# Folded output weights of a pooling mixer: split into float32r pairs when they are folded, two blocks before they are used

## The chip, the cores and the metric

The kernel runs on one core of one Trainium2 chip. The core has a matrix engine (PE in the profile, with its weight loads as PEld), a vector engine (DVE), a scalar engine (ACT), a general engine (POOL) and a sequencer that only issues transfers (SP). POOL and ACT can issue transfers too. The metric is device time of one execution in microseconds; the median of three runs of the kernel before is 907.18 us (906.41 to 909.01).

## The reference, cut to what matters

Inputs are x (4096 rows of 1024, float32) and the weights of one layer, a pooling mixer:

```python
normed = rms_norm(x, norm_w)
u, gate = split(normed @ in_w)                  # 1024 -> 2 x 1024
for g, win in enumerate((2, 4, 8, 16)):         # four groups of 256 channels
    pooled[g] = trailing_mean(u[g], win) - u[g]
    mixed[g] = pooled[g] @ group_w[g] + group_b[g]
y = mixed * scale * silu(gate)
h = x + y @ out_w
out = rms_norm(h, final_norm_w)
```

The float32 product is kept accurate by splitting each operand into a high part, rounded to the matrix engine's fast type float32r, and a low part, the rest. A product then takes three passes: high x high, high x low, low x high.

## The kernel before

Every large product is done by a seven-product scheme (Strassen in Winograd's form). The seven products are named P1 to P7. Each has its own weight matrix, a sum of quarters of the real weight, and its own operand, a sum of quarters of the activations, and the results are added up in PSUM banks or in SBUF. The order of the products is P1, P2, P7, P6, P5, P4, P3 in the input phases and P1, P7, P6, P2, P5, P4, P3 in the output phase.

There are three phases. In the first input phase ("a") one half of the input projection is done for four blocks of 1024 rows. In the second ("b") the other half is done for the same four blocks, with the operands that phase a stored to DRAM (`sd`). In the output phase ("o") the gated result, stored to DRAM as `yd`, goes through the output weight in eight blocks of 512 rows. A step is one product of one block. In phase b a step is 48 matrix instructions of 512 columns, but for P7 of blocks 1 to 3, which is itself split into seven small products (`product_seven`, line 745).

The list `steps` holds all steps, and the loop at line 1887 walks through it: it issues loads some steps ahead (`advance("load", ...)`), splits the operand of the next step or two (`split_step`), issues the matrix instructions and the read-out of the banks (`run`, `evict_in`), and then the extra work of that step. A scheduler with a model of its own decides how these instructions stand on each engine; `issue_after` bounds it. Each engine and each transfer queue works strictly in its order.

All loads and most temporaries share 11 slots named `st` and 8 named `vt`, 512 KB each (128 partitions x 4 KB). `take()` hands out the slot that was given back longest ago, and an instruction that writes into a slot waits until the last reader of the slot's old contents is done, a store to DRAM included. `ops` are four buffers for operands that are split, two a step. `w[i]` is the split weight of product i, 2 MB in two halves; it is the input weight until phase b ends, the output weight after it.

`out_w` is brought in during phase b. In block 1 `load_wo(0)` loads four quarters of one half of the rows after step P7, and `make_wo(0)` in step P6 scales them by `scale` (`scale_rows`, 8 ACT instructions) and stores seven folded matrices (`combine`: four DVE instructions; `store_weights`: seven stores to `wod` on SP). Block 2 does the same for the other half. In block 3, the last of phase b, as each product's input weight has been used for the last time, `load_w` loads the two halves of its output weight from `wod` (SP) and splits them (`split`: one ACT copy, one DVE subtraction) into `w[i]`. Pooling (`pool`, the running sums on DVE) is done a step or more after the projection that feeds it. In phase o some products are again split in seven with weights made from `wod[P2]` and `wod[P7]` (`load_inner`, `sum_inner`, `split_weight`).

In the row listings below `st8_97`, `op1_86` and the like are buffers (slot name and a running number), `sd2_1_1` is the saved operand of block 2, product 1, second half, `pair5_0` is the pair of product 5, first half, and the number of columns stands last.

Of the kernel before, what the change touches and what calls it, by code (L numbers as in the profile page):

```python
# [10 lines left out]
F32 = mybir.dt.float32  # L11
F32R = mybir.dt.float32r
# [3 lines left out]
P = 128  # L16
D = 1024
S = 4096
H = 512
TB = 1024  # L20
NB = S // TB
# [10 lines left out]
P1, P2, P3, P4, P5, P6, P7 = range(1, 8)  # L32
# [54 lines left out]
def kernel(  # L87
# [45 lines left out]
    dram = ctx.enter_context(tc.tile_pool(name="dram", bufs=1, space=bass.MemoryType.DRAM))  # L133
# [54 lines left out]
    def give(ap):  # L188
        next(p for p in (st, vt, early, early5) if id(ap) in p.used).give(ap)

    def add(dst, a, b):
        vector.tensor_tensor(out=dst, in0=a, in1=b, op=ALU.add)

    def sub(dst, a, b):
        return vector.tensor_tensor(out=dst, in0=a, in1=b, op=ALU.subtract)
# [4 lines left out]
    def copy(dst, src, func=AF.Copy):  # L200
        return scalar.activation(dst, src, func)

    def split(dst, src):

        latest_copy[0] = copy(dst[:, 0], src).ins
        latest_split[0] = sub(dst[:, 1], src, dst[:, 0].bitcast(F32)).ins

    latest_split, latest_copy = [None], [None]
# [9 lines left out]
    t3d = [dram.tile([P, 2, H], F32, name=f"t3d{h}") for h in range(2)]  # L218
    wod = {
        i: [dram.tile([P, 2, H], F32, name=f"wod{i}_{h}") for h in range(2)]  # L220
        for i in range(P1, P7 + 1)
    }
    sd = [
# [42 lines left out]
    def load_rows(mat, k, c):  # L266
        u = take()
        sync.dma_start(
            out=u, in_=mat[k * P : (k + 2) * P, c : c + H].rearrange("(t p) c -> p t c", p=P)
        )  # L270
        return u
# [9 lines left out]
    def scale_rows(u, cs):  # L281
        for j in range(2):
            scalar.activation(u[:, j], u[:, j], AF.Copy, scale=cs[j])
# [6 lines left out]
    def combine(b11, b21, b12, b22):  # L290

        sub(b12, b22, b12)
        add(b11, b12, b11)
        sub(b21, b21, b11)
        t1 = take()
        sub(t1, b22, b11)
        return {P6: b11, P7: b12, P5: t1, P4: b21, P3: b22}

    def pair(cs, h, kh):
        k = 4 * kh + 2 * h  # L300
        return cs[k : k + 2]

    def store_weights(dst, h, b11, b21, b12, b22):
        sync.dma_start(out=dst[P1][h], in_=b11)
        sync.dma_start(out=dst[P2][h], in_=b21)
        for i, u in combine(b11, b21, b12, b22).items():
            sync.dma_start(out=dst[i][h], in_=u)
            give(u)

# [66 lines left out]
    def load_wo(h):  # L376
        for n in range(2):
            for kh in range(2):
                raw_wo[kh, n] = load_rows(out_w, 4 * kh + 2 * h, n * H)

    def make_wo(h):
        us = dict(raw_wo)
        for (kh, n), u in us.items():
            scale_rows(u, pair(scale_c, h, kh))
        store_weights(wod, h, us[0, 0], us[1, 0], us[0, 1], us[1, 1])

    def load_w(src, i):
        for h in range(2):
            u = take()
            sync.dma_start(out=u, in_=src[i][h])  # L390
            with tc.issue_after(evicted[0]):
                split(w[i][h], u)
            give(u)

    latest = [None]

# [81 lines left out]
    sums, held = {}, {}  # L478
# [621 lines left out]
    ev, evicted, copied = {}, [None], []  # L1100
# [567 lines left out]
    def pool_later(n):  # L1668
        kind, b, i = steps[n]
        if i == P4:  # L1670
            args = (b, 0 if kind == "a" else 1, 1, ev.pop("22"), ev.pop("21"))
            wait = int(b == 0) if kind == "a" else 1 if b < NB - 1 else 2
        elif i == P3:
            args = (b, 0 if kind == "a" else 1, 0, ev.pop("12"), ev.pop("11"))
            wait = 1 + int(b == 0) if kind == "a" else 2 if b < NB - 1 else 5
        else:
            return
        pending.append((n + wait, args))

    def pool_due(n):  # L1680
        while pending and pending[0][0] <= n:
            pool(*pending.pop(0)[1])
# [169 lines left out]
    def advance(what, n, f, reach):  # L1852
        while at[what] + 1 < own_from and at[what] + 1 <= n + reach(*steps[at[what] + 1]):
            at[what] += 1
            f(at[what])
# [31 lines left out]
    for n in range(2, len(steps)):  # L1887
        kind, b, i = steps[n]
        ahead = kind == "a" and b + 1 < NB
        keep[0] = 5 if kind == "b" and b == NB - 1 else 3  # L1890
        advance("load", n, load, load_reach)
        if ahead:
            rows, squares = row_plan(b)
# [73 lines left out]
        if kind in ("a", "b"):  # L1967
            pool_later(n)
            if kind == "a":
                pool_due(n)  # L1970
            if kind == "b" and b == NB - 1:
                for p in {P1: (), P2: (), P7: (P1,), P6: (P2, P7), P5: (P6, P5)}.get(i, (i,)):
                    load_w(wod, p)
            if kind == "b" and b in (1, 2) and i == P7:
                load_wo(b - 1)
            if kind == "b" and b in (1, 2) and i == P6:
                with tc.issue_after(evicted[0]):
                    make_wo(b - 1)
            if kind == "b" and b == NB - 1 and i == P3:
                f = take("p (a b) -> p a b", a=2)  # L1980
                sync.dma_start(
                    out=f.rearrange("p a b -> p (a b)"), in_=final_w.partition_broadcast(P)
                )
                fw.append(f)
# [52 lines left out]
```

## Time and profile before

| | |
|---|---|
| median of three runs | 907.18 us |
| the profiled execution | 907.14 us, of which the span is 905.3 us |
| granted TensorE clock, mean | 0.998 |
| transfers | 203.30 MB, mean 225 GB/s |
| PE, DVE, ACT, POOL busy | 99%, 81%, 57%, 16% of the span |
| phase b, block 1: steps P6 to the end of block 2's P2 | 427.0 to 489.2 us |
| phase b, block 2: P6 to the end of block 3's P2 | 498.8 to 561.0 us |

The profile is one execution, taken by the hardware profiler. Times are microseconds from the start of the span. A busy figure is the union of an engine's instructions; those of the matrix engine are pipelined and overlap, so gaps shorter than one matrix instruction do not show as idle, while the distance from one instruction to the next still does. In a timeline row stand the start, the length, the engine, the line, the operation, what it writes and reads (buffer numbers left out) and the count; idle time ahead of it and what ended it stand in brackets. Nearly all DVE, ACT, POOL and SP rows carry line 79, a helper that records every call.

### The profile page before, as it was taken

The page shows a single profiled execution, that of the slowest core. Times are in us where ns is not written, and L with a number is a line of the kernel's source. Part 1 is how long each engine was busy: PE and PEld are TensorE (multiplying, and loading weights), DVE is VectorE, ACT ScalarE, POOL GpSimd, SP SyncE. Part 2 cuts the span into 40 slices and gives each one's busy share as a digit, 9 for nine tenths or more (in the row PEclk, how much of TensorE's full clock was granted, in tenths as well). Part 3 has the DMA queues.
Part 4 walks back from the last instruction along what each step waited for, and adds up shares of the span by engine and source line. Part 5 has one row for each costly group of instructions (what it writes and reads, how often), then busy time and mean ns, then how long its engine had stood idle before and what let it go on. Part 6 is the DMA issues. An engine that isn't in the chain of part 4 may idle for free.

```text
span 905.3 us, 12421 instructions
## 1 busy us (share of the span) xinstructions
PE 894.6 (99%) x4554; PEld 791.7 (87%) x4554; DVE 736.8 (81%) x910; ACT 518.6 (57%) x848; POOL 147.3 (16%) x244
## 2 busy tenths in 40 slices
PE   9999999999999999999999999999999999999996
PEld 7888888888888888889889889888889898998996
DVE  3899896984996997694596497699898878888798
ACT  7869547446445465346545644855557466565464
POOL 0031110110111000100010011011132343342430
PEclk9999999999999999999999999999999999999999
DMA  9989779677769565245574574756673855945953
GB/s 339 402 313 320 263 279 314 219 299 286 270 248 363 180 236 183 94 163 190 212 244 175 202 262 142 269 188 204 206 220 81 221 176 142 240 143 138 264 179 116
DMA packets 77756, 203.30 MB, mean 225 GB/s; under 512 B 7296, under 2 KB 25088, under 8 KB 77696
## 3 DMA queue, kind: packets, MB, share of 16 engines
q1 hardware_dynamic: 57872, 143.77, 46.0%
q0 software_dynamic: 19104, 57.69, 20.7%
q10 hardware_dynamic: 720, 1.06, 0.3%
q8 instruction: 35, 0.57, 0.3%
q14 instruction: 25, 0.20, 0.1%
HBM read 130.13 MB, written 72.36 MB: 224 GB/s over the span
## 4 chain that ended last, share of the span: by engine, by line
PE 50%; DVE 21%; DMA 10%; issue 6%; ACT 3%; POOL 1%; SPq 0%; DVEq 0%; POOLq 0%; ACTq 0%
PE bank L799 44%; DVE vt L79 8%; DVE st L79 6%; DVE op L79 5%; PE bank L745 3%; DMA vt<-yd 3%; PE bank L941 3%; DMA st<-wvd 2%; ACT op L79 1%; DMA st<-yd 1%; DVE w L79 1%; DMA out<-vt 1%; ACT vt L79 1%; DMA st<-wod 1%; DMA vt<-rd 1%
## 5 line engine op out<-in xcount | busy, mean ns | idle before, releaser
L799 PE MATMUL bank<-op,w 128*128 128x512 f32 x2544 | 550.6, 379 | 0.2 <-ACT st L79 0.2
L799 PEld LDWEIGHTS bank<-op,w 128*128 128x128 f32 x2544 | 480.4, 189 | 68.9 <-ACT st L79 0.6
L799 PE MATMUL bank<-w,op 128*128 128x512 f32 (+1 forms) x1044 | 230.5, 377 | 0.0
L799 PEld LDWEIGHTS bank<-w,op 128*128 128x128 f32 x1044 | 192.3, 189 | 25.0
L79 DVE TENSOR_TENSOR op<-st,op 128x1024 fp32r<-128x1024 f32 x120 | 145.9, 1220 | 60.1 <-ACT op L79 59.7
L79 ACT ACTIVATE op<-st 128x1024 fp32r<-128x1024 f32 x120 | 125.8, 1052 | 86.4 <-PE bank L799 31.2
L79 ACT ACTIVATE op<-vt 128x1024 fp32r<-128x1024 f32 x65 | 68.3, 1053 | 63.0 <-DVE vt L79 40.6
L79 ACT ACTIVATE vt<-bank 128x512 f32<-128x512 f32 (+1 forms) x122 | 67.4, 577 | 43.9 <-PE bank L799 37.8
L79 DVE TENSOR_TENSOR op<-vt,op 128x1024 fp32r<-128x1024 f32 x65 | 78.4, 1218 | 14.2 <-ACT op L79 14.1
L79 DVE TENSOR_TENSOR st<-st,st 128x1024 f32<-128x1024 f32 (+1 forms) x47 | 51.3, 1104 | 31.6 <-ACT st L79 16.8
L79 ACT ACTIVATE bank<-bank 128x512 f32<-128x512 f32 (+1 forms) x84 | 41.1, 490 | 53.1 <-PE bank L799 39.5
L79 POOL COPY vt<-tails 128x32 f32<-128x32 f32 x14 | 17.0, 1219 | 301.4 <-ACT tails L79 130.3
L79 ACT ACTIVATE st<-bank 128x512 f32<-128x512 f32 (+1 forms) x62 | 35.6, 588 | 37.5 <-PE bank L799 22.7
L79 DVE TENSOR_TENSOR vt<-bank,vt 128x512 f32<-128x512 f32 (+1 forms) x90 | 51.3, 596 | 6.0 <-PE bank L941 4.6
L79 ACT ACTIVATE st<-st 128x1024 f32<-128x1024 f32 x34 | 35.8, 1055 | 28.6 <-DVE st L79 27.1
L79 DVE TENSOR_TENSOR st<-bank,st 128x512 f32<-128x512 f32 (+1 forms) x72 | 43.7, 622 | 6.0 <-PE bank L941 3.1
L79 POOL DMA_DIRECT2D sd<-st x45 | 24.0, 535 | 125.1 <-DVE st L79 77.9
L941 PEld LDWEIGHTS bank<-w,op 128*128 128x128 f32 x312 | 40.4, 191 | 1.7
L79 DVE TENSOR_TENSOR st<-st,vt 128x1024 f32<-128x1024 f32 (+1 forms) x34 | 39.1, 1168 | 2.7 <-DMA vt<-rd 2.4
L941 PE MATMUL bank<-w,op 128*128 128x256 f32 x312 | 41.1, 275 | 0.0
L79 DVE TENSOR_TENSOR vt<-vt 128x1024 f32<-128x1024 f32 (+3 forms) x43 | 38.2, 890 | 0.2
L79 DVE TENSOR_TENSOR_SCAN vt<-vt,window 128x1040 f32<-128x1040 f32 x16 | 37.7, 2374 | 0.6 <-DMA wod<-vt 0.5
(118 smaller groups left out, 768.5 us busy)
## 6 DMA issues: line engine op xcount, KB each, us to landing
sd<-st POOLq DMA_DIRECT2D x45, 512.0 KB, 4.2
st<-sd SPq DMA_DIRECT2D x42, 512.0 KB, 4.0
st<-in_xt SPq DMA_DIRECT2D x28, 512.0 KB, 7.4
st<-in_x SPq DMA_DIRECT2D x21, 512.0 KB, 7.9
yd<-st SPq DMA_DIRECT2D x20, 512.0 KB, 3.3
vt<-yd SPq DMA_DIRECT2D x17, 512.0 KB, 10.5
st<-wod SPq DMA_DIRECT2D x16, 512.0 KB, 5.1
out<-vt POOLq DMA_DIRECT2D x16, 512.0 KB, 3.5
```

Of the source, the lines that this page charges most:

```text
L79: r = f(*args, **kwargs)
L745: latest[0] = nc.tensor.matmul(cell(n, c).rearrange("p (a s) -> p a s", s=2), x1, x2, start=i == P1 and k + m == 0, stop=k == 1 and m == 2 ...
L799: latest[0] = nc.tensor.matmul(ps, a, b, start=start and n == 0, stop=stop and n == 2, skip_group_check=True).ins
L941: latest[0] = nc.tensor.matmul(ps, x1, x2, start=start and k + n == 0, stop=k == 1 and n == 2, skip_group_check=True,).ins
```

## The change

In blocks 1 and 2 of phase b, the folded matrices are split where they are folded. `store_pair` takes a fresh slot for the high part (an ACT copy), makes the low part on DVE (in place of the source, or in a second fresh slot for P1 and P2, whose source is still needed), and stores both to a new DRAM tensor `pairs_d` on POOL's queue. The plain `wod` copies stay for P2 and P7 alone. `load_wo` moves from step P7 to P2, the scaling, the pairs of P1 and P2 and the fold from P6 to P7, and the other five pairs stand in step P6. In block 3 `load_w` loads each half of the pair, 1 MB, straight into `w[i]` from POOL's queue, without ACT or DVE; most products are loaded one step later than before. The number of slots that `take` keeps back in that block is 3 and no longer 5.

```diff
-        for i in range(P1, P7 + 1)
+        for i in (P2, P7)
+    }
+    pairs_d = {
+        i: [dram.tile([P, 2, 2, H], F32, name=f"pair{i}_{h}") for h in range(2)]
+        for i in range(P1, P7 + 1)
     }
...
-    def store_weights(dst, h, b11, b21, b12, b22):
-        sync.dma_start(out=dst[P1][h], in_=b11)
-        sync.dma_start(out=dst[P2][h], in_=b21)
-        for i, u in combine(b11, b21, b12, b22).items():
-            sync.dma_start(out=dst[i][h], in_=u)
-            give(u)
+    def store_pair(i, h, u, spare=False):
+        hi = take()
+        lo = take() if spare else u
+        latest_copy[0] = copy(hi.bitcast(F32R), u).ins
+        latest_split[0] = sub(lo.bitcast(F32R), u, hi).ins
+        for v, t in enumerate((hi, lo)):
+            gpsimd.dma_start(out=pairs_d[i][h][:, v], in_=t)
+            if spare or v == 0:
+                give(t)
+
+    def store_weights(h, b11, b21, b12, b22):
+        sync.dma_start(out=wod[P2][h], in_=b21)
+        store_pair(P1, h, b11, True)
+        store_pair(P2, h, b21, True)
+        return combine(b11, b21, b12, b22)
+
+    def store_rest(h, sums):
+        sync.dma_start(out=wod[P7][h], in_=sums[P7])
+        for i in (P6, P5, P4, P3, P7):
+            store_pair(i, h, sums[i])
+            give(sums[i])
...
-    def load_w(src, i):
+    def load_w(i):
         for h in range(2):
-            u = take()
-            sync.dma_start(out=u, in_=src[i][h])
-            with tc.issue_after(evicted[0]):
-                split(w[i][h], u)
-            give(u)
+            gpsimd.dma_start(out=w[i][h], in_=pairs_d[i][h].bitcast(F32R))
...
-        keep[0] = 5 if kind == "b" and b == NB - 1 else 3
+        keep[0] = 3
...
-                for p in {P1: (), P2: (), P7: (P1,), P6: (P2, P7), P5: (P6, P5)}.get(i, (i,)):
-                    load_w(wod, p)
-            if kind == "b" and b in (1, 2) and i == P7:
-                load_wo(b - 1)
-            if kind == "b" and b in (1, 2) and i == P6:
+                for p in {P1: (), P2: (P1,), P7: (P2,), P6: (P7,), P5: (P6,), P4: (P5,), P3: (P4, P3)}[i]:
+                    load_w(p)
+            if kind == "b" and b in (1, 2):
                 with tc.issue_after(evicted[0]):
-                    make_wo(b - 1)
+                    if i == P2:
+                        load_wo(b - 1)
+                    elif i == P7:
+                        folded = make_wo(b - 1)
+                    elif i == P6:
+                        store_rest(b - 1, folded)
```

How the instructions stand changes at three places that matter below. The first is ACT in block 1, right behind the read-out of step P7 (the four rows that read banks 0 to 3). Before, two operand copies and the read-out of step P6 (banks 4 to 7) come next, then the eight scalings:

```order
L79 ACTIVATE vt6_106<-bank3_72 128x512
L79 ACTIVATE op1_86<-st2_91 128x1024
L79 ACTIVATE op3_88<-st0_89 128x1024
L79 ACTIVATE st6_95<-bank4_73 128x512
L79 ACTIVATE st6_95<-bank5_74 128x512
L79 ACTIVATE st2_91<-bank6_75 128x512
L79 ACTIVATE st2_91<-bank7_76 128x512
L79 ACTIVATE vt1_101<-vt1_101,colt_114 128x512 x2
L79 ACTIVATE st1_90<-st1_90,colt_114 128x512 x2
L79 ACTIVATE st8_97<-st8_97,colt_114 128x512 x2
L79 ACTIVATE st9_98<-st9_98,colt_114 128x512 x2
```

In the changed kernel the scalings and the high parts of P1 (into `st8`) and P2 (into `st5`) stand there, and the operand copies and the read-out of P6 behind them:

```order
L79 ACTIVATE st0_89<-st0_89,colt_114 128x512 x2
L79 ACTIVATE vt7_107<-vt7_107,colt_114 128x512 x2
L79 ACTIVATE vt2_102<-vt2_102,colt_114 128x512 x2
L79 ACTIVATE vt0_100<-vt0_100,colt_114 128x512 x2
L79 ACTIVATE st8_97<-st0_89 128x1024
L79 ACTIVATE st5_94<-vt7_107 128x1024
L79 ACTIVATE op1_86<-st2_91 128x1024
L79 ACTIVATE st6_95<-bank4_73 128x512
L79 ACTIVATE st6_95<-bank5_74 128x512
L79 ACTIVATE op3_88<-vt6_106 128x1024
L79 ACTIVATE op0_85<-st1_90 128x1024
L79 ACTIVATE st2_91<-bank6_75 128x512
```

So the scalings moved ahead of P6's read-out, and two copies were added.

The second place is POOL's queue in block 1, the stores of the pairs of P6, P5, P4, P3 and P7. Before, nothing but small copies for the pooling stands there. Now:

```order
L79 DMA pair6_0_137<-vt3_103 128x1024
L79 DMA pair6_0_137<-st0_89 128x1024
L79 COPY vt6_106<-tails_116 128x2x16
L79 DMA pair5_0_135<-st0_89 128x1024
L79 DMA pair5_0_135<-st9_98 128x1024
L79 DMA pair4_0_133<-st0_89 128x1024
L79 DMA pair4_0_133<-vt7_107 128x1024
L79 DMA pair3_0_131<-st9_98 128x1024
L79 DMA pair3_0_131<-vt0_100 128x1024
L79 DMA pair7_0_139<-st0_89 128x1024
```

Slot `st0` carries, one after the other, the low part of P6 and the high parts of P5, P4 and P7; slot `st9` the low part of P5 and then the high part of P3.

The third place is DVE at the end of block 1: the low part of P3 and, three rows on, that of P7 (from `st0`), the adds that read out step P4 (banks 0 to 3), the first running sum, and the low part of the second half of block 2's first operand (`op0` from `st9`). Before, with no weight among them:

```order
L79 SCALAR_TENSOR_TENSOR vt7_107<-vt6_106,window_3432 128x1040
L79 TENSOR_TENSOR st6_95<-bank0_69,st6_95 128x512
L79 TENSOR_TENSOR st6_95<-bank1_70,st6_95 128x512
L79 TENSOR_TENSOR op3_88<-st8_97,op3_88 128x1024
L79 TENSOR_TENSOR st2_91<-bank2_71,st2_91 128x512
L79 SCALAR_TENSOR_TENSOR vt3_103<-vt3_103,vt0_100 128x2x512
L79 TENSOR_TENSOR st2_91<-bank3_72,st2_91 128x512
L79 TENSOR_TENSOR op0_85<-st1_90,op0_85 128x1024
```

and now:

```order
L79 TENSOR_TENSOR vt0_100<-vt0_100,st9_98 128x1024
L79 TENSOR_TENSOR st6_95<-bank0_69,st6_95 128x512
L79 TENSOR_TENSOR st6_95<-bank1_70,st6_95 128x512
L79 TENSOR_TENSOR vt2_102<-vt2_102,st0_89 128x1024
L79 TENSOR_TENSOR st2_91<-bank2_71,st2_91 128x512
L79 TENSOR_TENSOR st2_91<-bank3_72,st2_91 128x512
L79 SCALAR_TENSOR_TENSOR vt0_100<-vt1_101,window_3450 128x1040
L79 SCALAR_TENSOR_TENSOR vt0_100<-vt0_100,vt1_101 128x2x512
L79 TENSOR_REDUCE window_3588<-vt6_106 128x1
L79 SCALAR_TENSOR_TENSOR st6_95<-vt0_100,colt_114,st6_95 128x512
L79 TENSOR_TENSOR op0_85<-st9_98,op0_85 128x1024
```

Both running sums (of step P5's result) stood ahead of P4's read-out adds before; they stand behind those adds and the low part of P7 now.

More of the change, by code (lines that the diff above doesn't have):

```diff
@@ L384, in make_wo @@
             scale_rows(u, pair(scale_c, h, kh))
-        store_weights(wod, h, us[0, 0], us[1, 0], us[0, 1], us[1, 1])
-    def load_w(src, i):
+        return store_weights(h, us[0, 0], us[1, 0], us[0, 1], us[1, 1])
+    def load_w(i):
         for h in range(2):
-            u = take()
-            sync.dma_start(out=u, in_=src[i][h])
-            with tc.issue_after(evicted[0]):
-                split(w[i][h], u)
-            give(u)
+            gpsimd.dma_start(out=w[i][h], in_=pairs_d[i][h].bitcast(F32R))
     latest = [None]
```

## The prediction

> **What bounds the kernel now.** I read the page first, then PE's own waits, then the busy time by stretch, then the timelines of block 1.
>
> ```profile
> span 905.3 us, 12421 instructions
> PE 894.6 (99%) x4554; PEld 791.7 (87%) x4554; DVE 736.8 (81%) x910; ACT 518.6 (57%) x848; POOL 147.3 (16%) x244
> ...
> PE bank L941 <- DVE vt L79: 1.8, 1, 1.8
> PE bank L1687 <- PEq L2022: 0.8, 1, 0.8
> PE bank L451 <- DMA early<-in_group_w: 0.3, 1, 0.3
> PE bank L451 <- DMA early<-in_wut: 0.2, 1, 0.2
> PE bank L799 <- ACT st L79: 0.2, 1, 0.2
> ```
>
> PE is busy for all but 10.7 us of the span, and its five waits come to 3.3 us. Since gaps shorter than an instruction hide in "busy", I checked its pace:
>
> ```profile
> 427.04 62.33 PE L799 MATMUL bank<-op,w 128*128 128x512 f32 x288
> 489.20 2.84 PE L745 MATMUL bank<-op,w 128*128 128x256 f32 x24
> 498.80 21.53 PE L799 MATMUL bank<-op,w 128*128 128x512 f32 x99
> ```
>
> Six steps of 48 instructions take 489.20 - 427.04 = 62.16 us: 10.36 us a step, 0.216 us an instruction, the same from one end to the other. So blocks 1 and 2 of phase b run at PE's pace: what DVE and ACT do there is free while operands come in time, and costs one for one once they are late. There is one place where they are late:
>
> ```profile
> 565.00:650.00 85.00, 85.00 (x419) 75.05 (x417) 74.53 (x77) 50.58 (x72) 10.10 (x10) 1.00 0.70 223
> 650.00:660.00 10.00, 10.00 (x48) 8.77 (x47) 8.72 (x12) 7.08 (x15) 3.90 (x13) 1.00 0.27 106
> 660.00:670.00 10.00, 9.91 (x61) 8.76 (x59) 9.93 (x14) 8.20 (x13) 4.34 (x6) 1.00 0.86 239
> 670.00:680.00 10.00, 8.31 (x44) 7.49 (x45) 9.99 (x18) 2.42 (x4) 1.77 (x2) 1.00 0.96 252
> ...
> 671.69 0.94 PE L941 MATMUL bank<-inner,op 128*128 128x256 f32 x6 [1.77 <-DVE vt L79]
> ...
> L79 DVE TENSOR_TENSOR w<-st,w 128x1024 fp32r<-128x1024 f32 x14 | 16.5, 1217 | 5.5 <-ACT w L79 5.5
> L79 ACT ACTIVATE w<-st 128x1024 fp32r<-128x1024 f32 x14 | 14.3, 1059 | 3.6 <-DMA st<-wod 2.1 <-PE bank L799 1.4
> ```
>
> The columns of a stretch are PE, PEld, DVE, ACT and POOL busy, clock, DMA share, GB/s. DVE carries 74.53 of 85 us and then nearly all of 660 to 680, and PE waits 1.77 us for it. The 14 weight splits are 16.5 us of that backlog.
>
> **What the change gains.** The 14 copies and 14 subtractions leave block 3. The backlog shrinks by 16.5 us of work against a wait of 1.77 us, so I count the whole wait as gone: -1.8 us. More is not there to win: what else PE waits for lies at the start of the program (1.5 us), and the end behind the last product is not touched.
>
> **What it adds in blocks 1 and 2.** Seven copies of 1.05 us on ACT and seven subtractions of 1.22 us on DVE a block, 14 stores on POOL and five fewer on SP. As mere work it fits:
>
> ```profile
> 425.00:440.00 15.00, 15.00 (x80) 13.39 (x80) 6.09 (x6) 10.04 (x16) 0.00 (x0) 1.00 0.41 140
> 440.00:455.00 15.00, 15.00 (x71) 13.15 (x70) 11.77 (x12) 7.56 (x12) 0.21 (x1) 1.00 0.83 302
> 455.00:470.00 15.00, 15.00 (x72) 13.12 (x71) 15.00 (x18) 7.24 (x10) 2.12 (x1) 1.00 0.75 250
> 470.00:485.00 15.00, 15.00 (x71) 13.15 (x70) 14.68 (x17) 5.47 (x9) 1.35 (x2) 1.00 0.40 146
> 485.00:500.00 15.00, 15.00 (x111) 14.26 (x110) 7.01 (x8) 10.59 (x20) 0.00 (x0) 1.00 0.65 217
> ```
>
> DVE has 8.9 us free before 440 and 3.2 before 455. But from 455 to 485 it has only 0.3 us free in 30: a subtraction that slips past 455 pushes all behind it. What makes them slip is the slots. Slot st0 is P6's low part, then P5's, P4's and P7's high part, and each use waits until the store of the one before has landed. The price of a landing is the main unknown:
>
> ```profile
> sd<-st POOLq DMA_DIRECT2D x45, 512.0 KB, 4.2
> st<-sd SPq DMA_DIRECT2D x42, 512.0 KB, 4.0
> ...
> DMA to landing us min/median/max: 2.9/4.1/12.6
> ...
> sd<-st POOLq DMA_DIRECT2D x9, 512.0 KB, 4.0
> ...
> sd<-st POOLq DMA_DIRECT2D x7, 512.0 KB, 6.5
> ```
>
> The same kind of store (512 KB, POOL's queue) lands in 4.2 us in the median and 2.9 at least; the last two rows are the stretches 100 to 140 (263 GB/s) and 180 to 220 (310 GB/s). I first walk the chain at 4.2.
>
> ```profile
> 428.77 1.08 ACT L79 ACTIVATE op<-st 128x1024 fp32r<-128x1024 f32 x1
> 438.10 1.32 ACT L79 ACTIVATE vt<-vt,colt 128x512 f32<-128x512 f32 x2
> 439.32 3.78 ACT L79 ACTIVATE st<-st,colt 128x512 f32<-128x512 f32 x6
> 442.99 1.05 ACT L79 ACTIVATE op<-vt 128x1024 fp32r<-128x1024 f32 x1
> ...
> 443.13 1.23 DVE L79 TENSOR_TENSOR st<-st,st 128x1024 f32<-128x1024 f32 x1 [8.39 <-ACT st L79]
> 444.27 1.22 DVE L79 TENSOR_TENSOR op<-vt,op 128x1024 fp32r<-128x1024 f32 x1
> 453.66 4.68 DVE L79 TENSOR_TENSOR_SCAN vt<-vt,window 128x1040 f32<-128x1040 f32 x2
> 464.04 1.40 DVE L79 SCALAR_TENSOR_TENSOR st<-vt,colt,st 128x512 f32<-128x512 f32 x2
> 484.07 1.22 DVE L79 TENSOR_TENSOR op<-vt,op 128x1024 fp32r<-128x1024 f32 x1
> ```
>
> Block 1. ACT is through with P7's read-out at 428.8. The eight scalings take 442.99 - 438.10 = 4.9 us: 433.7. P1's high part is ready at 434.7 and its store, from st8, lands at 439.0. The low part of P2 goes into st8, so DVE waits there, with everything behind it. Six subtractions, 1.13 us apart, bring P6's low part at 445.9. From there, with 0.1 us a hand-over: landed 450.2, P5 high 451.4, landed 455.7, P4 high 456.8, landed 461.1, P7 high 462.3, P7 low 463.5. Behind it on DVE, up to the low part of the second operand that block 2's P7 needs at once, stand 4 running sums (2.34 each), 9 instructions of 1024 columns (1.13 apart) and 12 of 512 (0.66): 27.5 us, so 491.0. PE wants it at 489.3; before, it was there at 485.3. **Stall 1.7 us.** Two smaller ones lie within it or beside it: block 2's first operand (its second half is loaded into st9 only when P3's high part has landed) comes 0.4 us late, and P6's read-out on ACT, now behind the scalings, ends at about 437.2 where P5 first writes that bank at 437.4, which I count as nothing.
>
> Block 2 runs the same chain in st6, from PE's 498.80. P6's low part comes at 517.8 (the operand copy ahead of it needs a buffer that P5's first half holds until 514.3). Then landed 522.1, P5 high 523.3, landed 527.6, P4 high 528.7, landed 533.0, P7 high 534.2, P7 low 535.4; a read-out add, two gates, a running sum and the subtraction after it (6.1 us) bring DVE to 541.5, and the first operand of block 3, whose slot st8 was P3's high part until about 535, has its low half at 542.7. PE wants it at 498.80 + 4 x 10.36 + 0.1 = 540.3: 2.4 us, and 0.3 more for its second half. **Stall 2.7 us.** Together 4.4.
>
> Each further microsecond of landing adds 4 us in block 1 (P1, P6, P5, P4) and 3 in block 2, where P1's is hidden by the wait for the buffer. At the least, 2.9 us, both stalls are gone; at 6.5 us they are 10.9 and 9.6. Which is nearer? Block 1 moved 140, 302 and 250 GB/s in the three stretches from 425 to 470; nine more stores of 0.5 MB in these 45 us make it (231 + 100) = 331 GB/s, above the stretch with 6.5. But there the stores stood in pairs, while in the chain one goes at a time. I take 4.8, nearer the median: 1.7 + 2.4 + 2.7 + 1.8 = 8.6 us.
>
> On this the Trainium skill speaks against me: "DMA: Bandwidth & Descriptors", section "Anatomy of one DMA — SWDGE (gpsimd) path", gives a transfer from POOL's queue about 2.0 us plus its bytes at 436 GB/s, an estimate of 3.2 us for 512 KB. By that both stalls vanish and the time is that of the first rival below. The trace has 4.2 in the median and 2.9 at least, so I go by the trace.
>
> **Costed at nothing.** SP issues 24 fewer transfers. The 14 loads of 1 MB stand in POOL's queue behind PE's last use of each weight in block 3. The tightest is P3's, issued as phase o begins and used six steps later; a step of phase o is 24 instructions, so that is 6 x 24 x 0.216 = 31 us, against 8.4 us at twice the 512 KB landing. Without the cover a late one would cost up to those 8.4 us. Behind them in POOL's queue wait copies for the pooling and phase o's adds from x, which come a step or more later.
>
> **Sum.** 907.14 for the profiled execution (its span 905.3 and 1.8 around it), which is the median of the runs, 907.18, to 0.04: 907.1 - 1.8 + 8.6 = 914 us.
>
> **Rivals.** (a) *The landings are hidden.* At 3 us a landing, or if DVE's slack of 4 us before block 2's P7 is larger than I count, nothing is late, and the wait at 671 is gone: 907.1 - 1.8 = 905.4. For it: the minimum of 2.9, and DVE's 8.4 us of idling ahead of 443.13 that the change fills. Against it: four landings in a row, and 30 us of full DVE behind them. (b) *The transfers choke.* 16 MB more go through; landings of 6.5 us give 20.5 us of stalls, 926. For it: 0.83 and 0.75 DMA share already in block 1. Against it: stalls stretch the time in which the bytes move, which relieves the queue. (c) *The wait at 671 stays,* because not DVE's work but the loading of `wod[P2]` sets it: 914 + 1.8 = 916. Against it: those loads wait for slots that DVE frees late. That the splits don't really leave block 3 is not a rival; the order shows 14 loads into the weights with no arithmetic behind them.
>
> **Numbers.** Forecast (stalls of 4 to 14 us) 0.62; (a) 0.24; (b) 0.07; (c) 0.07. The time is 914; the range, from (a) to nearly (b), is 905 to 925; the forecast's own is 909.5 to 920. A measurement here can tell about 0.3%, 2.7 us, from no change. Faster by more than that needs more than the 1.8 us there is to win: 0.04, left for an effect that I don't see. Within: most of (a) and the low end of the forecast, 0.24. Slower: 0.72.
>
> **What would show it.** Right: PE waits on DVE or ACT at block 2's P1 or P7 and at block 3's P1, some 2 to 6 us each; ACT copies of high parts that wait for stores to the pairs; no wait near 671. Wrong: PE's six steps of blocks 1 and 2 still take 62.2 us each; or DVE has caught up by 485; or PE waits in phase o for a weight that POOL loaded.

## The result and the profile after

The changed kernel takes 939.98 us in the median of 4 runs (937.69 to 942.53), the kernel before beside it 907.26: a ratio of 1.036 [1.032, 1.040], 33 us slower. The direction was forecast, but the time lies well outside the range of 905 to 925. The profiled execution took 937.69 us. These are the head of its page, and the view of what PE waited for (total, times, longest):

```profile
span 935.9 us, 12450 instructions
PE 907.2 (97%) x4554; PEld 797.9 (85%) x4554; DVE 738.1 (79%) x910; ACT 518.3 (55%) x848; POOL 166.2 (18%) x286
...
PE bank L815 <- ACT op L79: 7.6, 3, 4.0
PE bank L957 <- DVE st L79: 3.7, 1, 3.7
PE bank L815 <- DVE op L79: 3.6, 4, 1.9
PE bank L815 <- ACT bank L79: 3.5, 1, 3.5
```

The span grew by 30.6 us; DVE and ACT are as busy as before (736.8 and 518.6 us then), since the splits were only moved. All of PE's waits sum to 21.5 us now (3.3 before). That is 18.2 of the 30.6; nearly all the rest stands in PE's busy time, which grew by 12.6 (907.2 against 894.6) with the same 4554 instructions. So the matmuls themselves have become slower somewhere. PE's timeline shows where the time is lost (L815 is the main product, L761 the seven small products of phase b, L957 those of phase o, called its own product below):

```profile
427.36 43.03 PE L815 MATMUL bank<-op,w 128*128 128x512 f32 x198
473.43 0.48 PE L815 MATMUL bank<-op,w 128*128 128x512 f32 x1 [3.04 <-ACT op L79]
474.69 14.69 PE L815 MATMUL bank<-op,w 128*128 128x512 f32 x59 [0.78 <-DVE op L79]
492.88 9.70 PE L815 MATMUL bank<-op,w 128*128 128x512 f32 x30 [3.50 <-ACT bank L79]
502.41 2.84 PE L761 MATMUL bank<-op,w 128*128 128x256 f32 x24
...
512.91 41.60 PE L815 MATMUL bank<-op,w 128*128 128x512 f32 x192
558.55 0.80 PE L815 MATMUL bank<-op,w 128*128 128x512 f32 x1 [4.04 <-ACT op L79]
...
584.90 2.84 PE L761 MATMUL bank<-op,w 128*128 128x256 f32 x24
...
613.32 25.95 PE L815 MATMUL bank<-op,w 128*128 128x512 f32 x119 [1.86 <-DVE op L79]
639.10 51.96 PE L815 MATMUL bank<-w,op 128*128 128x512 f32 x240
...
700.74 1.65 PE L957 MATMUL bank<-inner,op 128*128 128x256 f32 x6 [3.73 <-DVE st L79]
```

Against the same places before (427.04, 489.20, 498.80, 560.97, 612.01, 671.69, end 905.3), with the waits of the timeline subtracted:

| stretch | before | after | more | of it waits | rest |
|---|---|---|---|---|---|
| six steps from block 1's P6 to block 2's P7 | 62.16 | 75.05 | 12.89 | 7.32 | 5.57 |
| seven small products of block 2 | 9.60 | 10.50 | 0.90 | 0.63 | 0.27 |
| six steps to block 3's P7 | 62.17 | 71.99 | 9.82 | 5.49 | 4.33 |
| block 3's P7 to phase o | 51.04 | 54.20 | 3.16 | 2.36 | 0.80 |
| phase o to its own product | 59.68 | 61.64 | 1.96 | 1.96 | 0 |
| from there to the end | 233.61 | 235.16 | 1.55 | | 1.55 |

Another 0.32 us lies ahead of block 1's P6. The "rest" is mostly the clock: in rows of 1 us, with the granted clock at 0.50 for some 19 us in which PE works behind four of the waits, 9.7 us are lost. The remainder goes with stopping and starting: a matmul that stands alone between two waits takes 0.48 us (at 473.43) where one in a row takes 0.216. In the view by stretches of 5 us (PE with its count, PEld, DVE, ACT, POOL, granted clock, DMA share, GB/s), 15 to 17 matmuls stand behind a wait where 25 stand at full clock:

```profile
475.00:480.00 5.00, 5.00 (x17) 4.04 (x16) 5.00 (x6) 3.05 (x7) 0.00 (x0) 0.66 0.99 349
480.00:485.00 5.00, 5.00 (x25) 4.38 (x24) 5.00 (x5) 1.16 (x2) 0.00 (x0) 1.00 0.36 145
...
490.00:495.00 5.00, 2.12 (x5) 1.76 (x6) 5.00 (x6) 2.51 (x3) 0.09 (x1) 0.71 0.73 244
495.00:500.00 5.00, 5.00 (x15) 4.04 (x15) 2.96 (x6) 1.65 (x2) 0.33 (x1) 0.61 0.97 313
```

What made block 2's first product late stands in the timelines of ACT, DVE and SP (SPq is SP's DMA queue):

```profile
453.57 1.06 ACT L79 ACTIVATE st<-st 128x1024 fp32r<-128x1024 f32 x1 [3.65 <-DMA pair<-st]
...
458.01 1.06 ACT L79 ACTIVATE st<-vt 128x1024 fp32r<-128x1024 f32 x1 [2.32 <-DMA pair<-st]
...
472.32 1.06 ACT L79 ACTIVATE op<-st 128x1024 fp32r<-128x1024 f32 x1 [5.01 <-DMA st<-sd]
...
491.28 1.06 ACT L79 ACTIVATE op<-st 128x1024 fp32r<-128x1024 f32 x1 [7.76 <-DVE st L79]
492.25 0.58 ACT L79 ACTIVATE bank<-bank 128x512 f32<-128x512 f32 x1
...
463.80 1.22 DVE L79 TENSOR_TENSOR vt<-vt,st 128x1024 fp32r<-128x1024 f32 x1
...
468.88 2.38 DVE L79 TENSOR_TENSOR_SCAN vt<-vt,window 128x1040 f32<-128x1040 f32 x1 [2.67 <-DMA pair<-vt]
...
465.59 6.13 SPq L79 DMA_DIRECT2D st<-sd  x2
```

The high parts of P5 and P4 wait for stores to land, as forecast. The load of the operand's second half is issued at 465.59, when the store of P3's high part has freed its slot, and the ACT copy that needs it starts at 472.32. A running sum on DVE waits 2.67 us for the store of P3's low part, whose `vt` slot it writes. And at 491.28 ACT has waited 7.76 us for the front sum, which DVE makes from operands for the seven small products, with the copy of a bank behind it (492.25) for which PE waits 3.50 us: a place that the prediction doesn't have.

### The profile page after: what moved, and what is told of

The parts are those of the page before. It is cut to its first block, busy times and chain, and to the rows that moved or that the text cites. A ratio compares the mean times of both kernels' runs of the same rounds, so it can differ in the third digit from the quotient of the medians.

```text
span 935.9 us, 12450 instructions
## 1 busy us (share of the span) xinstructions
PE 907.2 (97%) x4554; PEld 797.9 (85%) x4554; DVE 738.1 (79%) x910; ACT 518.3 (55%) x848; POOL 166.2 (18%) x286
## 4 chain that ended last, share of the span: by engine, by line
PE 68%; issue 11%; DVE 9%; DMA 9%; POOL 1%; ACT 1%; DVEq 0%; POOLq 0%; SPq 0%; ACTq 0%
PE bank L815 60%; PE bank L957 4%; DVE vt L79 4%; PE bank L467 3%; DVE st L79 3%; DVE op L79 3%; DMA st<-yd 2%; DMA pair<-st 2%; DMA st<-sd 1%; DMA vt<-yd 1%; DMA st<-wod 1%; DMA yd<-vt 1%; POOL pair L79 1%; PE bank L761 1%; ACT st L79 1%
## 5 line engine op out<-in xcount | busy, mean ns | idle before, releaser
L815 PE MATMUL bank<-op,w 128*128 128x512 f32 x2544 | 560.7, 383 | 14.7 <-ACT op L79 7.6
L815 PEld LDWEIGHTS bank<-op,w 128*128 128x128 f32 x2544 | 485.1, 191 | 88.7 <-ACT op L79 9.1
L815 PE MATMUL bank<-w,op 128*128 128x512 f32 (+1 forms) x1044 | 231.2, 378 | 0.0
L815 PEld LDWEIGHTS bank<-w,op 128*128 128x128 f32 x1044 | 192.9, 190 | 25.2
L79 DVE TENSOR_TENSOR op<-vt,op 128x1024 fp32r<-128x1024 f32 x66 | 80.3, 1220 | 21.2 <-ACT op L79 21.2
L79 DVE TENSOR_TENSOR st<-st,st 128x1024 f32<-128x1024 f32 (+2 forms) x41 | 45.5, 1128 | 31.9 <-DMA st<-yd 13.6
L79 DVE TENSOR_TENSOR vt<-bank,vt 128x512 f32<-128x512 f32 (+1 forms) x111 | 62.1, 590 | 9.4 <-PE bank L957 3.8
L79 ACT ACTIVATE st<-st 128x1024 f32<-128x1024 f32 (+2 forms) x40 | 41.3, 1034 | 33.6 <-DVE st L79 23.9
L79 POOL COPY vt<-tails 128x32 f32<-128x32 f32 x14 | 12.9, 920 | 196.4 <-ACT tails L79 106.8
L957 PEld LDWEIGHTS bank<-w,op 128*128 128x128 f32 x312 | 40.3, 191 | 1.9 <-ACT bank L79 0.3
L957 PE MATMUL bank<-w,op 128*128 128x256 f32 x312 | 41.2, 275 | 0.0
L79 DVE TENSOR_TENSOR st<-st,vt 128x1024 f32<-128x1024 f32 (+2 forms) x31 | 36.0, 1183 | 6.3 <-DMA st<-wod 3.4
L79 DVE TENSOR_TENSOR st<-bank,st 128x512 f32<-128x512 f32 (+1 forms) x51 | 32.6, 652 | 5.6 <-PE bank L957 3.0
L957 PE MATMUL bank<-inner,op 128*128 128x256 f32 x234 | 32.3, 279 | 3.7 <-DVE st L79 3.7
```

Of the source, the lines that this page charges most:

```text
L79: r = f(*args, **kwargs)
L815: latest[0] = nc.tensor.matmul(ps, a, b, start=start and n == 0, stop=stop and n == 2, skip_group_check=True).ins
L957: latest[0] = nc.tensor.matmul(ps, x1, x2, start=start and k + n == 0, stop=k == 1 and n == 2, skip_group_check=True,).ins
```

## The experiments

Theory A: the slots. Every use of a slot waits for the landing of the store before it, and the stalls come from that. Theory B: the transfers; 14 MB of stores in two blocks crowd out the operand loads. Theory C: the work; ACT and DVE have no room for 14 splits. Each ratio is against the kernel before on the same chip, with its 95% interval.

**1. Slots free.** The arithmetic stays, but the stores read a tile that nobody is changing.

```diff
         for v, t in enumerate((hi, lo)):
-            gpsimd.dma_start(out=pairs_d[i][h][:, v], in_=t)
+            gpsimd.tensor_copy(out=scrap, in_=t[:, 0, 0:1])
+            gpsimd.dma_start(out=pairs_d[i][h][:, v], in_=w[P1][h][:, 0].bitcast(F32))
```

> The changed kernel, but the 28 stores of pairs read one fixed weight tile instead of the slots that hold the parts; POOL reads one column of each part first, so a store is issued no earlier than before. Arithmetic, bytes and issue places stay; a slot is free as soon as its part is computed, without waiting for a landing. The pairs in memory, and so phase o's weights and the output, are not the reference's. Theory A (slots: each part waits for the landing of a store in the same slot, and the stalls follow from it): blocks 1 and 2 cost at most 2 us more than before, and with some 5 us behind 585 us that this run does not touch, 907 to 914 us. Theory B (transfers: 14 MB more in two blocks crowd out the operand loads): 928 us or more. Theory C (work: 14 copies and 14 subtractions more on ACT and DVE): 925 to 935 us.

Measured: 935.8 us, 1.031 [1.030, 1.033]. The number seems to speak for B or C, but the edit did something else than I meant: since nothing tied the stores to the parts any more, all 28 were issued between 285 and 332 us. PE's timeline has a loss there, and hardly any in the blocks in question:

```profile
310.50 17.28 PE L816 MATMUL bank<-op,w 128*128 128x512 f32 x71 [1.86 <-DVE op L79]
...
336.15 89.19 PE L816 MATMUL bank<-op,w 128*128 128x512 f32 x405 [7.30 <-DVE op L79]
...
514.61 62.33 PE L816 MATMUL bank<-op,w 128*128 128x512 f32 x288
576.77 2.84 PE L762 MATMUL bank<-op,w 128*128 128x256 f32 x24
```

From 514.61 to 576.77 six steps take 62.16 us, exactly as before the change, with all of block 2's splits in them. Block 1's six steps take 62.82 us, with one wait of 0.39. Theory C falls: the work fits. The burst costs some 13 us in another place, before block 1, where DVE waits 4.85 and 4.50 us for loads that came late; another 12.9 us are lost behind block 3's P7, where the loads of pairs and the number of slots kept back are still those of the changed kernel.

**2. Slots free, stores in their place.** The same, with each store made to follow POOL's one-column read.

```diff
+            seen_by = gpsimd.tensor_copy(out=scrap, in_=t[:, 0, 0:1]).ins
+            with tc.issue_after(seen_by):
+                gpsimd.dma_start(out=pairs_d[i][h][:, v], in_=w[P1][h][:, 0].bitcast(F32))
```

> As the run with free slots before it, but each store is now held in its place: it follows POOL's one-column read of the part that it stands for. It reads one fixed weight tile, so a slot is free once the part is computed, and the bytes still move in blocks 1 and 2. The pairs, phase o's weights and the output are not the reference's. Theory A (slots: what waits is the next use of a slot, for the landing of the store before): no wait of ACT or DVE on pair stores, stalls of blocks 1 to 3 under 4 us together instead of 16, 909 to 917 us. Theory B (transfers: the bytes make the operand loads late whatever the slots do): block 2's first product and block 3's first product still wait 3 us or more each, 928 to 940.

Measured: 921.84 us, 1.016 [1.014, 1.018]: 18.1 us less than the changed kernel. The transfers from 425 to 485 (KB each, median us from issue to landing) and PE's timeline:

```profile
pair<-w POOLq DMA_DIRECT2D x14, 512.0 KB, 8.8
st<-sd SPq DMA_DIRECT2D x8, 512.0 KB, 8.2
```

```profile
501.27 62.33 PE L817 MATMUL bank<-op,w 128*128 128x512 f32 x288
563.44 0.27 PE L763 MATMUL bank<-op,w 128*128 128x256 f32 x1
...
623.64 51.96 PE L817 MATMUL bank<-w,op 128*128 128x512 f32 x240
```

A landing takes 8.8 us, against 4.0 (10 stores from `st`) and 6.1 (4 from `vt`) in the changed kernel, and an operand load 8.2 against 4.7. Yet up to block 3's P7 PE waits only 0.39 us in block 1's P5 and 0.63 in block 2's small products. So the bytes alone do not make PE wait there, though they make every landing longer: A and not B, for these blocks. The time is above A's 909 to 917 because of what comes behind: 60.2 us from 563.44 to phase o, against 51.04 before, and a wait of 3.48 near 685.

**3. No loads of pairs.** Block 3 loads no weights for phase o; the stores stay.

```diff
-                for p in {P1: (), P2: (P1,), P7: (P2,), P6: (P7,), P5: (P6,), P4: (P5,), P3: (P4, P3)}[i]:
-                    load_w(p)
+                pass
```

> The changed kernel without the 14 loads of pairs into the weights in block 3: phase o multiplies by block 3's weights, so the output is not the reference's. The stores stay. All theories: the lateness up to block 3's P7 stays, some 24 us. If the loads (14 MB between 575 and 640 us) make block 3's and phase o's operands late, the 3.5 us that are lost between block 3's P7 and phase o, and the 2 us more at the wait before 700, go: 931 to 935 us. If they are hidden, as forecast: 938 to 941.

Measured: 936.9 us, 1.032 [1.030, 1.034], and 51.05 us from block 3's P7 to phase o: the 3.1 us of that stretch are the loads. The wait near 700 stays (3.57 us), so that one is not theirs. The time lies between the two that were expected: the loads were not hidden, but they cost less than the 5.5 us put down to them.

**4. Thin stores, no loads.** A thin store leaves most of a pair unwritten, so the loads of pairs are left out here too; the run to hold it against is run 3.

```diff
-            gpsimd.dma_start(out=pairs_d[i][h][:, v], in_=t)
+            gpsimd.dma_start(out=pairs_d[i][h][:, v, :, 0:32], in_=t[:, :, 0:32])
```

> The changed kernel, with stores of 32 of 512 columns from the same slots, and without the 14 loads of pairs in block 3 (phase o multiplies by block 3's weights; the output is not the reference's). To be held against the run without loads, 936.9 us. Theory A (slots and landings): the wait for a landing stays, shorter by what the bytes cost; if a landing without bytes takes 2 us or more, the chain of four still makes the parts some 8 us late, and one stall of 1 to 3 us stays: 911 to 922. Theory B (transfers): nothing is late any more, and only the wait near 700 us is left: 908 to 912.

Measured: 919.33 us, 1.014 [1.012, 1.016], 17.6 us less than run 3. Landings are at 2.6 us, below the 2.9 at which the prediction saw no stall, but the six steps still have two: one in block 1's P5, one at the place of the 3.50 of the changed kernel:

```profile
pair<-st POOLq DMA_DIRECT2D x10, 32.0 KB, 2.6
...
441.25 43.00 PE L815 MATMUL bank<-op,w 128*128 128x512 f32 x198 [1.12 <-ACT st L79]
487.39 6.74 PE L815 MATMUL bank<-op,w 128*128 128x512 f32 x30 [3.14 <-ACT bank L79]
```

Waiting without bytes costs 4.3 us here (some 0.4 of it stands in run 2 too), bytes without waiting (run 2) cost 0.4. Taking away either one gives back some 18 us, so the two are not separate shares: the slots make everything wait for landings, and the bytes make the landings long. That is A, with the bytes as what sets its price.

**5 and 6. A delay of known size in the kernel before.** The low part of both halves of block 2's first operand is computed twice (run 5) or three times (run 6), so DVE is late by 2 or 4 instructions.

```diff
+        for _ in range(1 + again[0]):
             latest_split[0] = sub(dst[:, 1], src, dst[:, 0].bitcast(F32)).ins
...
+        again[0] = 2 if q and (b, i) == (2, P1) else 0
         t = split_halves(s[key], None if q or later else sd[b].get(i))
+        again[0] = 0
```

> The kernel before, with the subtraction of the low part of each half of block 2's first operand done twice (same result): two instructions of 1.13 us ahead of a product that had no slack, so PE should wait 2.0 to 2.3 us at 469 us. If a wait costs its length and nothing more: 909 to 909.5 us. If every wait also slows the matmuls behind it: 911 or more. From the waits of 1.8 and 1.9 us without and 3.0 us and more with a lower clock behind them I expect no slowing at this length.

> The same with the subtractions done three times: four instructions, PE waits 4.2 to 4.6 us in one or two pieces. If a wait costs its length alone: 911.3 to 911.8 us. If a wait above some 3 us is followed by matmuls at a lower granted clock, as behind the waits of 3.0, 3.5 and 4.0 us in the changed kernel: 2 to 4 us more, 913 to 916, with the clock at 0.5 to 0.7 in the 5 us behind the wait.

Measured: 908.32 us, 1.001 [1.000, 1.003], and 912.37 us, 1.006 [1.004, 1.008]. The wait is not at block 2's first product, where I put it. These are PE and ACT, first of run 5, then of run 6:

```profile
484.11 6.74 PE L803 MATMUL bank<-op,w 128*128 128x512 f32 x30 [0.48 <-ACT bank L79]
```

```profile
486.48 8.43 PE L803 MATMUL bank<-op,w 128*128 128x512 f32 x30 [3.59 <-ACT bank L79]
...
484.88 1.06 ACT L79 ACTIVATE op<-st 128x1024 fp32r<-128x1024 f32 x1 [7.85 <-DVE st L79]
```

So block 2 has its tightest date at the copy of the seven products' front sum on ACT, ahead of a bank copy that PE needs: two more subtractions of 1.13 us on DVE nearly fit, four do not. (The profiled executions are at the slow end of both runs; they also wait 2.19 and 1.91 us at the own product.) Behind the short wait 30 matmuls take 6.74 us, behind the long one 8.43, with the clock at 0.73 and 0.93 in the two stretches of 5 us there. The wait of 3.59 thus costs 1.7 us more than its length.

**7. Slots free, no loads.** Runs 2 and 3 together.

> The run with free slots and stores held in place, 921.8 us, now also without the 14 loads of pairs in block 3 (stores read a fixed tile, phase o multiplies by block 3's weights; the output is not the reference's). In that run 60.0 us passed from block 3's P7 to phase o, against 50.7 before: if the loads are what costs this, by making operands of block 3 late, it comes back to 51 and the time to 911 to 914 us. If the loads are hidden and something else delays block 3 (work on DVE, the rotation of slots): 919 to 922. The waits in the seven small products (0.6 us each) and near 680 us are not touched.

Measured: 914.09 us, 1.007 [1.005, 1.010], 51.97 us from block 3's P7 to phase o, about as expected if the loads are the cause. They cost 7.8 us where nothing ahead of them stalls, and 3.1 in the changed kernel.

**8. Five slots kept back, as before.**

```diff
-        keep[0] = 3
+        keep[0] = 5 if kind == "b" and b == NB - 1 else 3
```

> The changed kernel with the number of vt slots that block 3 leaves free set back to 5, as before. The wait near 700 us (3.73 us, and some 1.7 us of lower clock behind it) is on a load of a sum of P7 that stands on SP's queue behind a load of x that needs a vt slot. If the rotation of slots makes that wait, it changes with this number: under 2 us, and 935 to 938 us in all. If DVE's work or the bytes make it: unchanged, 939 to 941.

Measured: 930.14 us, 1.025 [1.024, 1.027]: 9.8 us less, more than I expected, for an edit of one number.

```profile
556.11 0.48 PE L815 MATMUL bank<-op,w 128*128 128x512 f32 x1 [3.89 <-ACT op L79]
...
583.62 2.84 PE L761 MATMUL bank<-op,w 128*128 128x256 f32 x24
...
634.91 51.96 PE L815 MATMUL bank<-w,op 128*128 128x512 f32 x240
...
693.12 0.94 PE L957 MATMUL bank<-inner,op 128*128 128x256 f32 x6 [0.31 <-DVE vt L79]
```

The stalls of blocks 2 and 3 stay, the wait at 613 us is gone (51.29 us to phase o), and the one at the own product is 0.31 us, with full clock behind it. From block 3's P7 to the end it is 7.2 us shorter; the other 1.3 us of the 8.5 between the two profiled spans lie ahead, where this number does nothing. So 7.2 us are its price, and the 9.8 between the medians hold some scatter.

**9. One product a step.** P7 and P6 are split and stored in step P6, then P5, P4 and P3 each in its own.

```diff
-                    elif i == P6:
-                        store_rest(b - 1, folded)
+                    elif i in (P6, P5, P4, P3):
+                        store_rest(b - 1, folded, (P7, P6) if i == P6 else (i,))
```

> The changed kernel with the five pairs of a half split and stored one product to a step (P7 and P6 in step P6, then P5, P4, P3), instead of all in step P6. Theory A (each part waits for the landing before it): with 10 us between parts no landing is waited for, and the stalls of blocks 2 and 3 shrink to under 6 us with their lower clock; the sums hold their slots longer, which may cost operand loads 2 to 5 us: 912 to 925. If the stalls come from DVE and ACT being full just ahead of the blocks' ends, parts split later make them worse: 940 or more.

Measured: 937.68 us, 1.032 [1.030, 1.035]; both expectations missed. The sums hold their slots up to three steps longer now. One ACT copy waits 9.54 us for an operand load (at 462.77), one of the subtractions for the seven products 6.29 us for a store to land (at 567.39), and PE waits 4.23, 3.22 and, among block 3's small products, 5.45 us. So spreading the five does not help: the waits move to other users of the slots. That it is the longer hold of the sums which makes them wait is likely, but no run shows it alone.

**10. Only P1 and P2 as pairs**, at the places of the change, with five slots kept back; the other five are stored as sums and split in block 3.

```diff
-            store_pair(i, h, sums[i])
+            sync.dma_start(out=wod[i][h], in_=sums[i])
```

> Only P1 and P2 are split and stored as pairs in blocks 1 and 2, where they were in the changed kernel; the other five are stored as sums and split in block 3 as before. The chain of five pairs in one slot is gone; 4 of 14 splits and 8 of 28 stores of pairs stay. Theory A: no stall in blocks 1 and 2 over 1 us, 905 to 909. Theories B and C: about 4/14 of the 33 us, 914 to 919.

Measured: 911.62 us, 1.005 [1.003, 1.006], above the 905 to 909 of theory A and below the 914 to 919 of the others. No stall in the six steps of blocks 1 and 2 (62.28 and 62.16 us), as A has it. What is left are the 0.63 us waits in the small products and 2.83 at the own product; they explain the profiled execution (909.4, the fastest of seven), not the 2 us that the median lies above it.

**11. The same two pairs at the old places:** load in step P7, fold and store in P6.

> The kernel before, with the pairs of P1 and P2 alone, at the places where it loads and folds (load in block b's step P7, fold and store in step P6), and 5 vt slots as before. Where the version with these two pairs at the changed places had 911.6 us, its 0.6 us waits in the seven small products should go, since the raw weights take their four slots a step later. With 4 of 14 splits out of block 3, the wait at 671 us (1.77) shrinks if DVE's work sets it: 904.5 to 906.5. If it is the load of a sum of P7, as in the changed kernel: 907 to 909.

Measured: 924.88 us, 1.019 [1.017, 1.020]: 13 us worse than run 10; both times that were expected are missed.

```profile
486.58 8.43 PE L821 MATMUL bank<-op,w 128*128 128x512 f32 x30 [2.93 <-ACT bank L79]
...
577.89 1.65 PE L767 MATMUL bank<-op,inner 128*128 128x256 f32 x6 [8.06 <-ACT st L79]
...
451.09 1.06 ACT L79 ACTIVATE vt<-st 128x1024 fp32r<-128x1024 f32 x1 [4.40 <-DMA pair<-vt]
...
577.46 0.38 ACT L79 ACTIVATE st<-bank 128x256 f32<-128x256 f32 x1 [8.45 <-DMA yd<-st]
```

P2's high part waits 4.40 us for the landing of one of P1's parts, and block 3's small products wait 8.06 us for a slot that is free only when a store of `yd` out of it has landed; what made that store late is not shown. The two runs differ only in where the raw weights are loaded and the pairs made, so with the same eight stores one place has no stall in these steps and the other costs 13 us more.

**12. All three undone:** slots free, no loads, five slots kept back; splits and stores stay.

> Three parts undone at once: slots free without waiting for landings (stores read a fixed tile, held in place), no loads of pairs in block 3, and 5 vt slots left free in block 3 as before. The 14 splits and 14 MB of stores in blocks 1 and 2 stay; the output is not the reference's. Alone, they gave back 18, 3 (8 where nothing stalls ahead of them) and 10 us of 33. If these are all the causes: the waits left are the 0.6 us ones in the seven small products, 905 to 909 us. If the splits as work or the stores as bytes cost anything of their own: 912 or more.

Measured: 909.62 us, 1.0017 [1.0006, 1.0027], 1.6 us over the kernel before and 0.6 above what was expected if these are all the causes. Undone one after another, slots give 18.1 us, loads 7.8, the number of slots kept back 4.5, and 1.6 are left, in which the small products' waits (0.63, 0.63 and 1.10 us) lie: 32.0 in all, against 32.7 measured. None of the versions beats the kernel before.

## Why the prediction was right and wrong

**The bound and the work: right.** PE sets the pace of these blocks, and 14 splits and 18 more stores cost next to nothing as work (block 2 in run 1, and run 12).

**The chain of slots: right in time, too narrow.** The forecast had P7's low part done at 463.5 with landings of 4.2 us, which is 465.9 with the 4.8 that it then took; it was done at 465.02. Single landings differ: 6.8 us pass from the store of P6's low part (446.75) to the start of P5's copy, and 3.0 from P5's store (455.04) to P4's copy; the sum hardly does. What failed is the step from there to PE, "Stall 1.7 us" at block 2's P7 (4.1 with the longer landings): there is no wait at that product, and 7.32 us ahead of it. I followed four parts in one slot and then counted DVE's instructions behind them. But every other user of such slots waits too: the running sum (2.67 us), and SP's operand loads, so that block 2's first operand, "0.4 us late", made PE wait 3.04 and 0.78. The load itself took 6.7 us, not 4.2, with the DMA share at 1.01 from 465 to 470. And P7 is not the tightest date: that is the copy of the front sum on ACT, with the bank copy behind it (runs 5 and 6). So also "at the least, 2.9 us, both stalls are gone" is wrong (run 4: landings of 2.6 us and still 3.14 us of waiting at the front sum), and rival (a) with it. The Trainium skill, "DMA: Bandwidth & Descriptors", section "Anatomy of one DMA — SWDGE (gpsimd) path", has 2.0 us plus bytes at 436 GB/s; that makes an estimate of 2.1 us for 32 KB, where run 4 shows 2.6, and the 3.2 for 512 KB stand against 4.0 to 8.8 here.

**Block 3's first product: right in place, near in size.** Forecast 2.7 + 1.8 = 4.5 us of waits, measured 5.49. The low half of that operand was done at 559.75, where the forecast, moved by the 14.1 us by which block 2 began late, has 558.6. But the load of the operand's half that PE waits for first was late as well: ACT waits 3.60 us for it (at 557.45), and PE 4.04 for ACT. Two paths are late together here; the sum had one, so that the size came near is in part luck.

**A wait costs its length ("costs one for one"): wrong.** The sum added stalls as they are. Behind the longer waits the clock falls to half, and 9.7 of the 30.6 us are that (most of the 5.57, 4.33 and 1.55 in the table). The waits of blocks 2 and 3 alone, 12.8 us where I took 8.6, would have made it 918, inside the range.

**"So I count the whole wait as gone": wrong for the change, right for the splits.** The wait at 671 became 3.73 us. With five slots kept back it is 0.31 (run 8; 0.32 in run 12), so without the splits it does go. With ten of the 14 splits left it was no shorter than before (2.83 and 2.11 in runs 10 and 11). The change also lowers the number of slots kept back; I quoted that edit and never priced it. With 3, the second half of P7's sum is loaded late, behind a load of x in SP's queue, and DVE waits 3.45 us for it. These are the changed kernel's load and wait, and then the same load in run 8, where it is the last of `wod`:

```profile
688.28 0.32 SPq L79 DMA_DIRECT2D st<-wod  x1
696.06 0.69 DVE L79 TENSOR_TENSOR st<-st,vt 128x512 f32<-128x512 f32 x1 [3.45 <-DMA st<-wod]
```

```profile
665.45 0.32 SPq L79 DMA_DIRECT2D vt<-wod  x1
```

Rival (c) was near: a load sets the wait, though of P7's sum and not P2's, and it costs more than the 1.8 us that were to be won. This missing term is 7.2 us, or 4.5 once the other two are undone.

**The loads of pairs, "costed at nothing": wrong.** I asked when the weights are needed, and none was late. I did not ask what 14 loads of 1 MB, twice the bytes of those before, do to the others. From 570 to 650 us:

```profile
w<-pair POOLq DMA_DIRECT2D x14, 1024.0 KB, 7.8
st<-yd SPq DMA_DIRECT2D x4, 512.0 KB, 8.0
vt<-yd SPq DMA_DIRECT2D x4, 512.0 KB, 12.0
```

The loads of phase o's operands need 8 and 12 us there, and 4.7 and 5.1 without the loads of pairs (run 3). Before the change they were long too, 7.0 and 11.3 us, and PE did not wait; so a long landing need not do harm. What does it here is one load, issued at 593.27, for which DVE waits until 610.90, with PE's wait at 613 behind it. These are that wait, and the same one in run 3, which is over at 600.47:

```profile
610.90 1.23 DVE L79 TENSOR_TENSOR st<-st,st 128x1024 f32<-128x1024 f32 x1 [13.57 <-DMA st<-yd]
```

```profile
600.47 1.23 DVE L79 TENSOR_TENSOR st<-st,st 128x1024 f32<-128x1024 f32 x1 [2.55 <-DMA st<-yd]
```

Rival (b), the choking transfers, was right here (3 to 8 us). In blocks 1 and 2, where I had it, bytes cost time only through the landings that the slots wait for (runs 2 and 4).

**P6's read-out, costed at nothing:** nothing in the changed kernel, 0.4 us in run 2 and 1.12 in run 4, where on DVE the low part of P2's weight stands ahead of an operand's. The two waits of 0.63 us in the small products were not foreseen; the ACT copy ahead of each goes into a slot that DVE is still reading, and waits 1.02 us for it.

What stays open: the wait at 613 goes both without the loads (run 3) and with five slots kept back (run 8), and how the two act together is not settled; that is why the three shares depend on the order in which they are undone. A version with its own buffers for the high parts was not tried.

## What to carry to other kernels

Where slots rotate, a store is a hold on its slot until it lands; list every later user of that slot on every queue, loads and in-order engines too, before a chain is priced, and price each number in the diff that steers the rotation. A transfer that comes in time itself can still make the others late. And on PE, a wait from some 2 us up may cost twice: once as itself, and once as matmuls at half clock behind it.

## What the runs showed of the hardware

The granted clock behind a wait is 0.50 in steps of 1 us, for 3 to 4 us or some multiple of it, and then 1.00 again; nothing between lasts. In these profiles it fell behind (or already during) all 18 waits of 3.48 us and more, and behind 10 of the 17 from 1.77 to 3.34 us: a wait of 1.86 at 310 us in run 1 has it, 1.77 before the change, 1.86 at 613 and 3.14 in run 4 have not. Half clock for 3.4 us costs 1.7, as in run 6. The Trainium skill, "TensorE: Matmul & The Clock Gate", section "Part 1: The HAM clock gate (the "warmup" mystery)", describes half clock after an idle window of about 3.4 us and full clock after a busy one, with windows that run freely; the traces agree on the half and on the length, and differ in that waits of 1.9 us can already do it. Its remark that the ramp is under 1% of a typical kernel span is about the start of a kernel. Read as a price for stalls it would have one leave the clock out; here that is 9.7 of 935.9 us, small in the span and a third of the loss.
